# A row softmax on one core: five pieces per tile for four, with the scaling shared by VectorE and ScalarE

## The chip, the core and the metric

The kernel runs on one core of a Trainium2 chip. The metric is the device time of one execution in microseconds (us). The engines that compute here are VectorE (DVE in the profile) and ScalarE (ACT). SyncE (SP) computes nothing; it issues the transfers between the chip's main memory and SBUF, the on-chip memory of 128 partitions. Each engine runs its own list of instructions in order, and the engines wait for each other through semaphores. The transfers of SyncE's queue are worked off by sixteen DMA engines.

## The reference

The input is 16 x 256 rows of 32768 float32 numbers. Each row is divided by the temperature, which is 1.0 here, and put through a softmax:

```python
scaled = logits / temperature
scaled = scaled - scaled.max(axis=-1, keepdims=True)
exp_scaled = np.exp(scaled)
return (exp_scaled / exp_scaled.sum(axis=-1, keepdims=True)).astype(np.float32)
```

That is 537 MB read and 537 MB written, with one exponential for each number.

## The kernel before

A row of 32768 is cut into two halves, and each half lies on a partition of its own. So the 4096 rows become 8192 half rows of `_W` = 16384 columns, and these make `G` = 64 tiles of 128 partitions. A tile is 8.4 MB. SBUF holds three of them in one tensor `X`, which the profile calls xs (`_BUFS` = 3, tile g in slot g modulo 3), and everything is computed in place.

`compute(g)` (line 120) writes down the work of a tile. It treats the tile as `K` = 4 pieces of `_PIECE` = 4096 columns.

- Line 133: VectorE takes the negated maximum of each piece into the small tensor `t`. The first of these waits for the tile's load.
- Line 146: ScalarE takes the exponential of the piece in place, with that maximum as bias, and adds up the piece's sum on the way (the accumulator read that the profile shows as an instruction of its own).
- Lines 157 to 186 join the pieces. A shuffle fetches the numbers of the neighbouring partition, which holds the other half of the row (157). VectorE takes the maximum over all pieces of the row (161). ScalarE turns the differences of the maxima into a factor for each piece, `ee` (168). VectorE multiplies factors and sums and adds them up (174), and takes the reciprocal into `row` (186).
- Line 193: VectorE multiplies each piece in place by its factor and by the reciprocal, as two per-partition scalars of one instruction.

`Stream` wraps an engine with a semaphore: `done` counts an instruction, `wait` makes the engine wait for counts, and leaves out what it has waited for before. `hist` holds, for each tile, the instructions that the tile two later must wait for, as the small tensors exist twice.

`transfers(n)` (line 61) is the order of the transfers, all issued by SyncE: three loads first, then store and load by turns. In the steady part the plan reads: load i, store i-1, load i+1, store i. A load (line 214) waits until the store of the tile three before has finished, since it uses its slot. A store (line 223) waits for the scaling of all pieces that it covers (`overlapping`). Most transfers are a whole tile. Tile 0's store and tile 3's load come in halves, and the last tile is stored in quarters of `_LAST_STORE` = 4096 columns.

Of the kernel before, what the change touches and what calls it, by code (L numbers as in the profile page):

```python
# [7 lines left out]

_W = 16384
_BUFS = 3  # L10
_PIECE = 4096
_LAST_STORE = 4096


class Stream:


    def __init__(self, nc, engine, name):
        self.engine = engine
        self.sem = nc.alloc_semaphore(name)  # L20
        self.count = 0
        self.seen = {}
# [38 lines left out]
def transfers(n):  # L61
    half = _W // 2
    whole = [(0, _W)]
    halves = [(0, half), (half, half)]
    quarters = [(s, _LAST_STORE) for s in range(0, _W, _LAST_STORE)]
    plan = [("L", 0, whole), ("L", 1, whole), ("L", 2, whole)]
    plan += [("S", 0, halves), ("L", 3, halves), ("S", 1, whole), ("S", 2, whole)]
    for i in range(4, n - 2):
        plan += [("L", i, whole), ("S", i - 1, whole)]
    plan += [("L", n - 2, whole), ("L", n - 1, whole)]  # L70
    plan += [("S", n - 3, whole), ("S", n - 2, whole), ("S", n - 1, quarters)]
    return plan


@with_exitstack
def kernel(
    ctx: ExitStack,
    tc: tile.TileContext,
    logits: bass.AP,
    temperature: bass.AP,  # L80
    out: bass.AP,
):
    nc = tc.nc
    inv_t = 1.0 / float(temperature)
    P = nc.NUM_PARTITIONS
    fp32 = mybir.dt.float32
    Exp = mybir.ActivationFunctionType.Exp
    A = mybir.AluOpType

    xf = logits.flatten_outer_dims()  # L90
    of = out.flatten_outer_dims()
    N, V = xf.shape
    assert V == 2 * _W and (N * 2) % P == 0
    x = xf.rearrange("n (h v) -> (n h) v", h=2)
    o = of.rearrange("n (h v) -> (n h) v", h=2)
    G = N * 2 // P
    K = _W // _PIECE
    swap = [i ^ 1 for i in range(32)]

    ctx.enter_context(tc.tile_critical())  # L100
    X = nc.alloc_sbuf_tensor("xs", [P, _BUFS * _W], fp32)
    T = [nc.alloc_sbuf_tensor(f"t{q}", [P, 4 * K], fp32) for q in range(2)]
    E = [nc.alloc_sbuf_tensor(f"ee{q}", [P, 2 * K], fp32) for q in range(2)]
    J = [nc.alloc_sbuf_tensor(f"junk{q}", [P, 2 * K], fp32) for q in range(2)]
    R = [nc.alloc_sbuf_tensor(f"row{q}", [P, 4], fp32) for q in range(2)]

    sp = Stream(nc, nc.sync, "sp")
    dve = Stream(nc, nc.vector, "dve")
    act = Stream(nc, nc.scalar, "act")
    loads = Lanes(nc, "ld")  # L110
    stores = Lanes(nc, "st")
    landed = {}
    stored = {}
    scaled = {}
    hist = {}

    def overlapping(parts, s, n):
        return [token for (a, m), token in parts.items() if a < s + n and s < a + m]

    def compute(g):  # L120
        base = (g % _BUFS) * _W
        t, e, j_, r = T[g % 2], E[g % 2], J[g % 2], R[g % 2]
        tv = t[:, 0 : 4 * K].rearrange("p (a b k) -> p a b k", a=2, b=2)
        old = hist.get(g - 2)
        if old:
            dve.wait(*old)
        sums = None
        for k in range(K):
            s = k * _PIECE
            xs = X[:, base + s : base + s + _PIECE]  # L130
            dve.wait(*overlapping(landed[g], s, _PIECE))
            m = dve.done(
                nc.vector.tensor_reduce(  # L133
                    out=t[:, k : k + 1], in_=xs, axis=mybir.AxisListType.X, op=A.max, negate=True
                )
            )
            if inv_t != 1.0:
                dve.wait(m)
                m = dve.done(
                    nc.vector.tensor_scalar_mul(  # L140
                        out=t[:, k : k + 1], in0=t[:, k : k + 1], scalar1=inv_t
                    )
                )
            act.wait(m)
            sums = act.done(
                nc.scalar.activation(  # L146
                    out=xs,
                    in_=xs,
                    func=Exp,
                    bias=t[:, k : k + 1],  # L150
                    scale=inv_t,
                    accum_out=t[:, K + k : K + k + 1],
                )
            )
        dve.wait(sums)
        sh = dve.done(
            nc.vector.stream_shuffle(out=t[:, 2 * K : 4 * K], in_=t[:, 0 : 2 * K], mask=swap)  # L157
        )
        dve.wait(sh)
        mx = dve.done(  # L160
            nc.vector.tensor_reduce(  # L161
                out=r[:, 0:1], in_=tv[:, :, 0, :], axis=mybir.AxisListType.XY, op=A.min
            )
        )
        act.wait(mx)
        ev = e[:, 0 : 2 * K].rearrange("p (a k) -> p a k", a=2)
        ee = act.done(
            nc.scalar.activation(  # L168
                out=ev, in_=tv[:, :, 0, :], func=Exp, bias=r[:, 0:1], scale=-1.0
            )  # L170
        )
        dve.wait(ee)
        tr = dve.done(
            nc.vector.tensor_tensor_reduce(  # L174
                out=j_[:, 0 : 2 * K].rearrange("p (a k) -> p a k", a=2),
                in0=ev,
                in1=tv[:, :, 1, :],
                scale=1.0,
                scalar=0.0,
                op0=A.mult,  # L180
                op1=A.add,
                accum_out=r[:, 1:2],
            )
        )
        dve.wait(tr)
        rc = dve.done(nc.vector.reciprocal(out=r[:, 2:3], in_=r[:, 1:2]))  # L186
        dve.wait(rc)
        scaled[g] = {}
        for k in range(K):
            s = k * _PIECE  # L190
            xs = X[:, base + s : base + s + _PIECE]
            scaled[g][s, _PIECE] = dve.done(
                nc.vector.tensor_scalar(  # L193
                    out=xs,
                    in0=xs,
                    scalar1=e[:, k : k + 1],
                    scalar2=r[:, 2:3],
                    op0=A.mult,
                    op1=A.mult,
                )  # L200
            )
        hist[g] = (ee, tr)

    for what, g, parts in transfers(G):
        base = (g % _BUFS) * _W
        rows = slice(g * P, (g + 1) * P)
        if what == "L":
            landed[g] = {}
            for k, (s, n) in enumerate(parts):
                if g >= _BUFS:  # L210
                    sp.wait(*overlapping(stored[g - _BUFS], s, n))
                landed[g][s, n] = loads.add(
                    (g % _BUFS, k),
                    nc.sync.dma_start(out=X[:, base + s : base + s + n], in_=x[rows, s : s + n]),
                )
            compute(g)
        else:
            stored[g] = {}
            for k, (s, n) in enumerate(parts):
                sp.wait(*overlapping(scaled[g], s, n))  # L220
                stored[g][s, n] = stores.add(
                    (g % _BUFS, k),
                    nc.sync.dma_start(out=o[rows, s : s + n], in_=X[:, base + s : base + s + n]),  # L223
                )
    sp.wait(*stores.tokens())
# [35 lines left out]
```

## Time and profile before

| What | Value |
|---|---|
| Median of 3 runs | 2512.25 us (2511.07 to 2513.49) |
| The profiled execution's own time | 2513.76 us |
| Its span in the profile | 2512.0 us |
| Mean rate of the transfers over the span | 427 GB/s |
| Bytes moved | 1073.86 MB |
| Load, from issue to landing, median of 63 | 46.1 us |
| Whole-tile store, from issue to landing, median of 62 | 26.7 us |

The busy times of the engines are sums over the whole span. A group's row shows the source line, the engine, the operation, what it writes and reads, the number of instructions, then busy time in us and the mean of one in ns, and last how long the engine had sat idle just before such instructions and who ended that. A row of the timeline shows start and duration in us, with equal neighbours merged (x4 is four instructions). A row of a window shows its ends, its length, the busy time of each engine with its instructions, the clock, the share of the DMA engines' time, and GB/s. A packet of the DMA counts where it starts, so short windows are coarse. SPq is the queue of SyncE.

### The profile page before, as it was taken

How to read it: one execution, taken by the hardware profiler on the slowest of the kernel's cores; microseconds unless marked ns; L12 is line 12 of the kernel's file. 1: busy time of each engine (PE TensorE's matmuls, PEld its weight loads, DVE VectorE, ACT ScalarE, POOL GpSimd, SP SyncE). 2: the span in 40 equal slices, each digit the busy share in tenths (PEclk: the TensorE clock that was granted, in tenths of full speed). 3: DMA queues.
4: the chain of work that ended last, by engine and by line, in shares of the span. 5: the costliest groups of instructions: out<-in, count | busy, mean ns of one | idle time of the engine just before them, and what ended most of it. 6: DMA issues, size and time to landing. Idle time of an engine off the chain costs nothing.

```text
span 2512.0 us, 1661 instructions
## 1 busy us (share of the span) xinstructions
DVE 1755.7 (70%) x896; ACT 993.5 (40%) x577; POOL 0.2 (0%) x4
## 2 busy tenths in 40 slices
DVE  5866676766767667677676766777767676676776
ACT  3443342433424334243342433424334244342443
POOL 0000000000000000000000000000000000000000
DMA  9999999999999999999999999999999999999999
GB/s 409 443 427 432 434 432 432 425 432 432 420 433 425 429 431 422 432 424 430 433 421 431 434 427 425 434 431 422 433 432 421 431 422 433 433 420 432 434 420 389
DMA packets 19165, 1073.86 MB, mean 427 GB/s; under 512 B 2128, under 2 KB 2128, under 8 KB 2128
## 3 DMA queue, kind: packets, MB, share of 16 engines
q1 hardware_dynamic: 19152, 1073.75, 99.8%
q14 instruction: 13, 0.11, 0.0%
HBM read 536.87 MB, written 536.87 MB: 427 GB/s over the span
## 4 chain that ended last, share of the span: by engine, by line
DMA 57%; DVE 36%; ACT 5%; SPq 0%; issue 0%
DMA xs<-in_logits_dram 56%; DVE t L133 23%; DVE xs L193 12%; ACT xs L146 5%; DMA out_dram<-xs 1%; ACT ee L168 0%; SPq L223 0%; DVE row L186 0%; DVE row L161 0%; DVE t L157 0%; DVE junk L174 0%; DVE row L174 0%; SPq L256 0%; SPq L100 0%
## 5 line engine op out<-in xcount | busy, mean ns | idle before, releaser
L146 ACT ACTIVATE xs<-xs,t 128x4096 f32<-128x4096 f32 x256 | 949.2, 3708 | 1464.4 <-DVE t L133 1464.4
L133 DVE TENSOR_REDUCE t<-xs 128x1 f32<-128x4096 f32 x256 | 1113.4, 4412 | 462.1 <-DMA xs<-in_logits_dram 462.1
L193 DVE TENSOR_SCALAR xs<-xs,ee,row 128x4096 f32<-128x4096 f32 x256 | 600.4, 2409 | 2.3
L157 DVE LOAD_MASK_SELECT t<-t x64 | 0.9, 14 | 248.1 <-ACT xs L146 248.1
L146 ACT ACTIVATION_READ_ACCUMULATOR xs<-xs,t 128x1 f32 x256 | 47.7, 186 | 0.0
L168 ACT ACTIVATE ee<-t,row 128x8 f32<-128x8 f32 x64 | 19.2, 301 | 27.6 <-DVE row L161 27.6
L174 DVE CUSTOM_DVE_ANT_1 junk<-ee,t 128x8 f32<-128x8 f32 x64 | 10.7, 167 | 23.6 <-ACT ee L168 23.6
L186 DVE RECIPROCAL row<-row 128x1 f32<-128x1 f32 x64 | 10.5, 164 | 2.2
L161 DVE TENSOR_REDUCE row<-t 128x1 f32<-128x8 f32 x64 | 10.3, 161 | 2.2
L157 DVE STREAM_SHUFFLE t<-t 128x8 f32<-128x8 f32 x64 | 10.2, 160 | 0.0
L174 DVE DVE_READ_ACCUMULATOR2_ANT row<- 128x1 f32 x64 | 5.3, 83 | 0.0
L146 ACT ACT_TABLE_LOAD x1 | 1.3, 1283 | 0.9 <-SPq L100 0.9
L242 POOL MEMSET const-bfloat16-1.0<- 128x1 bf16 x1 | 0.1, 101 | 0.0
L242 POOL MEMSET const-uint8-127<- 128x1 uint8 x1 | 0.1, 101 | 0.0
L242 POOL MEMSET const-float32-0.0<- 128x1 f32 x1 | 0.1, 98 | 0.2 <-issue 0.2
L242 POOL MEMSET const-float32-1.0<- 128x1 f32 x1 | 0.1, 98 | 0.0
## 6 DMA issues: line engine op xcount, KB each, us to landing
out_dram<-xs SPq DMA_DIRECT2D x2, 4096.0 KB, 25.1
xs<-in_logits_dram SPq DMA_DIRECT2D x2, 4096.0 KB, 19.3
out_dram<-xs SPq DMA_DIRECT2D x4, 2048.0 KB, 10.8
xs<-in_logits_dram SPq DMA_DIRECT2D x63, 46.1
out_dram<-xs SPq DMA_DIRECT2D x62, 26.7
```

The lines of the kernel that those rows point to most:

```text
L133: nc.vector.tensor_reduce(out=t[:, k : k + 1], in_=xs, axis=mybir.AxisListType.X, op=A.max, negate=True)
L146: nc.scalar.activation(out=xs, in_=xs, func=Exp, bias=t[:, k : k + 1], scale=inv_t, accum_out=t[:, K + k : K + k + 1],)
L157: nc.vector.stream_shuffle(out=t[:, 2 * K : 4 * K], in_=t[:, 0 : 2 * K], mask=swap)
L161: nc.vector.tensor_reduce(out=r[:, 0:1], in_=tv[:, :, 0, :], axis=mybir.AxisListType.XY, op=A.min)
L168: nc.scalar.activation(out=ev, in_=tv[:, :, 0, :], func=Exp, bias=r[:, 0:1], scale=-1.0)
L174: nc.vector.tensor_tensor_reduce(out=j_[:, 0 : 2 * K].rearrange("p (a k) -> p a k", a=2), in0=ev, in1=tv[:, :, 1, :], scale=1.0, scalar=0. ...
L186: rc = dve.done(nc.vector.reciprocal(out=r[:, 2:3], in_=r[:, 1:2]))
L193: nc.vector.tensor_scalar(out=xs, in0=xs, scalar1=e[:, k : k + 1], scalar2=r[:, 2:3], op0=A.mult, op1=A.mult,)
L242: nc = _bacc.Bacc("TRN2", target_bir_lowering=False, num_devices=1)
```

## The change

Each tile is treated as five pieces, of 4096, 4096, 4096, 2560 and 1536 columns. The maxima and exponentials run over these five. After the reciprocal, a new small VectorE instruction multiplies the five factors by it, into the tensor `junk` (128x5). The scaling then multiplies each piece by this one product: pieces 0, 1 and 4 on VectorE, pieces 2 and 3 on ScalarE (`_ON_ACT`), side by side. A store waits for whichever of the two engines its pieces need. The small tensors grow from four entries to five for each group, and `hist` now also holds the scaling instructions. The plan of transfers, their sizes and the buffers are as before. `compute` is divided into the methods of a class `Tile`, called in the same order.

```diff
-_PIECE = 4096
+_PIECES = (4096, 4096, 4096, 2560, 1536)
+_ON_ACT = (2, 3)
...
-    K = _W // _PIECE
+    K = len(_PIECES)
+    starts = [sum(_PIECES[:k]) for k in range(K)]
...
+        def piece(self, k):
+            s = self.base + starts[k]
+            return X[:, s : s + _PIECES[k]]
+
+        def exponentials(self, k):
+            t = self.t
+            if k == 0 and self.g >= 2:
+                dve.wait(*hist[self.g - 2])
+            xs = self.piece(k)
+            dve.wait(*overlapping(landed[self.g], starts[k], _PIECES[k]))
...
-        for k in range(K):
-            s = k * _PIECE
-            xs = X[:, base + s : base + s + _PIECE]
-            scaled[g][s, _PIECE] = dve.done(
-                nc.vector.tensor_scalar(
-                    out=xs,
-                    in0=xs,
-                    scalar1=e[:, k : k + 1],
-                    scalar2=r[:, 2:3],
-                    op0=A.mult,
-                    op1=A.mult,
-                )
-            )
-        hist[g] = (ee, tr)
+        def scale(self):
+            f = self.j
+            w = dve.done(
+                nc.vector.tensor_scalar_mul(out=f[:, 0:K], in0=self.e[:, 0:K], scalar1=self.r[:, 2:3])
+            )
+            act.wait(w)
+            dve.wait(w)
+            for k in range(K):
+                xs = self.piece(k)
+                if k in _ON_ACT:
+                    token = act.done(nc.scalar.mul(out=xs, in_=xs, mul=f[:, k : k + 1]))
+                else:
+                    token = dve.done(
+                        nc.vector.tensor_scalar_mul(out=xs, in0=xs, scalar1=f[:, k : k + 1])
+                    )
+                scaled[self.g][starts[k], _PIECES[k]] = token
+            hist[self.g] += tuple(scaled[self.g].values())
+
+    def compute(g):
+        a = Tile(g)
         for k in range(K):
...
+            a.exponentials(k)
+        a.totals()
+        a.scale()
```

More of the change, by code (lines that the diff above doesn't have):

```diff
@@ L96 @@
     G = N * 2 // P
-    K = _W // _PIECE
+    K = len(_PIECES)
+    starts = [sum(_PIECES[:k]) for k in range(K)]
+    assert sum(_PIECES) == _W
     swap = [i ^ 1 for i in range(32)]
@@ L118, in overlapping, with __init__ @@
         return [token for (a, m), token in parts.items() if a < s + n and s < a + m]
[L120 to L127, printed above, removed]
-        for k in range(K):
-            s = k * _PIECE
-            xs = X[:, base + s : base + s + _PIECE]
-            dve.wait(*overlapping(landed[g], s, _PIECE))
+    class Tile:
+        def __init__(self, g):
+            self.g = g
+            self.base = (g % _BUFS) * _W
+            self.t, self.e, self.j, self.r = T[g % 2], E[g % 2], J[g % 2], R[g % 2]
+            self.tv = self.t[:, 0 : 4 * K].rearrange("p (a b k) -> p a b k", a=2, b=2)
+            self.sums = None
+            scaled[g] = {}
+        def piece(self, k):
[7 more added lines that the diff above has]
+            dve.wait(*overlapping(landed[self.g], starts[k], _PIECES[k]))
             m = dve.done(
@@ L144, in compute @@
             act.wait(m)
-            sums = act.done(
+            self.sums = act.done(
                 nc.scalar.activation(
@@ L154, in compute @@
             )
-        dve.wait(sums)
-        sh = dve.done(
-            nc.vector.stream_shuffle(out=t[:, 2 * K : 4 * K], in_=t[:, 0 : 2 * K], mask=swap)
-        )
[L159 to L162, printed above, removed]
-            )
-        )
[L165 to L179, printed above, removed]
-                op0=A.mult,
[L181 to L191, printed above, removed]
-            scaled[g][s, _PIECE] = dve.done(
-                nc.vector.tensor_scalar(
-                    out=xs,
-                    in0=xs,
-                    scalar1=e[:, k : k + 1],
-                    scalar2=r[:, 2:3],
-                    op0=A.mult,
-                    op1=A.mult,
-                )
-            )
-        hist[g] = (ee, tr)
+        def totals(self):
+            t, e, r, tv = self.t, self.e, self.r, self.tv
+            dve.wait(self.sums)
+            sh = dve.done(
+                nc.vector.stream_shuffle(out=t[:, 2 * K : 4 * K], in_=t[:, 0 : 2 * K], mask=swap)
+            )
+            dve.wait(sh)
+            mx = dve.done(
+                nc.vector.tensor_reduce(
+                    out=r[:, 0:1], in_=tv[:, :, 0, :], axis=mybir.AxisListType.XY, op=A.min
+                )
+            )
+            act.wait(mx)
+            ev = e[:, 0 : 2 * K].rearrange("p (a k) -> p a k", a=2)
+            ee = act.done(
+                nc.scalar.activation(
+                    out=ev, in_=tv[:, :, 0, :], func=Exp, bias=r[:, 0:1], scale=-1.0
+                )
+            )
+            dve.wait(ee)
+            tr = dve.done(
+                nc.vector.tensor_tensor_reduce(
+                    out=self.j[:, 0 : 2 * K].rearrange("p (a k) -> p a k", a=2),
+                    in0=ev,
+                    in1=tv[:, :, 1, :],
+                    scale=1.0,
+                    scalar=0.0,
+                    op0=A.mult,
+                    op1=A.add,
+                    accum_out=r[:, 1:2],
+                )
+            )
+            dve.wait(tr)
+            rc = dve.done(nc.vector.reciprocal(out=r[:, 2:3], in_=r[:, 1:2]))
+            dve.wait(rc)
+            hist[self.g] = (ee, tr)
@@ new lines, in scale @@
+        def scale(self):
+            f = self.j
+            w = dve.done(
+                nc.vector.tensor_scalar_mul(out=f[:, 0:K], in0=self.e[:, 0:K], scalar1=self.r[:, 2:3])
+            )
+            act.wait(w)
[7 more added lines that the diff above has]
+                        nc.vector.tensor_scalar_mul(out=xs, in0=xs, scalar1=f[:, k : k + 1])
+                    )
+                scaled[self.g][starts[k], _PIECES[k]] = token
+            hist[self.g] += tuple(scaled[self.g].values())
@@ L204 @@
+    def compute(g):
+        a = Tile(g)
+        for k in range(K):
+            a.exponentials(k)
+        a.totals()
+        a.scale()
     for what, g, parts in transfers(G):
```

## The prediction, made before the changed kernel ran

> **What bounds the kernel now.** I read the page's shares and transfer rows first, then the grouped waits, then one tile in the timeline, then the DMA rate in long windows, and last the end of the run.
>
> ```profile
> span 2512.0 us, 1661 instructions
> DVE 1755.7 (70%) x896; ACT 993.5 (40%) x577; POOL 0.2 (0%) x4
> q1 hardware_dynamic: 19152, 1073.75, 99.8%
> L146 ACT ACTIVATE xs<-xs,t 128x4096 f32<-128x4096 f32 x256 | 949.2, 3708 | 1464.4 <-DVE t L133 1464.4
> L133 DVE TENSOR_REDUCE t<-xs 128x1 f32<-128x4096 f32 x256 | 1113.4, 4412 | 462.1 <-DMA xs<-in_logits_dram 462.1
> L193 DVE TENSOR_SCALAR xs<-xs,ee,row 128x4096 f32<-128x4096 f32 x256 | 600.4, 2409 | 2.3
> L168 ACT ACTIVATE ee<-t,row 128x8 f32<-128x8 f32 x64 | 19.2, 301 | 27.6 <-DVE row L161 27.6
> L186 DVE RECIPROCAL row<-row 128x1 f32<-128x1 f32 x64 | 10.5, 164 | 2.2
> L161 DVE TENSOR_REDUCE row<-t 128x1 f32<-128x8 f32 x64 | 10.3, 161 | 2.2
> SPq L223 <- DVE xs L193: 2385.7, 68, 47.6
> ```
>
> The only data queue is busy for 99.8% of sixteen engines' span, while VectorE works 70% and ScalarE 40%. So 0.2% of 2512.0, about 5 us, is all the idle DMA time there is. The last row, SyncE's wait for the scaling, looks alarming (2385.7 us) but is only the place where an early engine parks. Whether it costs anything is read from one tile:
>
> ```profile
> 2355.05 17.40 DVE L133 TENSOR_REDUCE t<-xs 128x1 f32<-128x4096 f32 x4 [7.07 <-DMA xs<-in_logits_dram]
> 2359.50 3.71 ACT L146 ACTIVATE xs<-xs,t 128x4096 f32<-128x4096 f32 x1 [21.35 <-DVE t L133]
> 2372.48 3.71 ACT L146 ACTIVATE xs<-xs,t 128x4096 f32<-128x4096 f32 x1 [0.53 <-DVE t L133]
> 2376.10 0.19 ACT L146 ACTIVATION_READ_ACCUMULATOR xs<-xs,t 128x1 f32 x1
> 2376.33 0.16 DVE L157 STREAM_SHUFFLE t<-t 128x8 f32<-128x8 f32 x1
> 2377.26 0.16 DVE L186 RECIPROCAL row<-row 128x1 f32<-128x1 f32 x1
> 2377.46 9.38 DVE L193 TENSOR_SCALAR xs<-xs,ee,row 128x4096 f32<-128x4096 f32 x4
> 2386.86 0.33 SPq L223 DMA_DIRECT2D out_dram<-xs  x1
> 2387.24 0.43 SPq L214 DMA_DIRECT2D xs<-in_logits_dram  x1
> 2394.01 4.42 DVE L133 TENSOR_REDUCE t<-xs 128x1 f32<-128x4096 f32 x1 [7.17 <-DMA xs<-in_logits_dram]
> ```
>
> A tile takes 2386.86 - 2355.05 = 31.81 us from landing to store. At that moment the previously issued load is still coming: it lands 7.15 us later, and VectorE idles those 7.17 us. The store and the next load join a queue that is not empty. So the period is set by transfers, and compute has 7 us to spare as the last DMA engine sees it.
>
> The early engines may see less. The rate falls after some twelve tiles:
>
> ```profile
> 161.73 8.75 DVE L133 TENSOR_REDUCE t<-xs 128x1 f32<-128x4096 f32 x2 [12.07 <-DMA xs<-in_logits_dram]
> 473.79 8.75 DVE L133 TENSOR_REDUCE t<-xs 128x1 f32<-128x4096 f32 x2 [6.84 <-DMA xs<-in_logits_dram]
> 2432.70 8.74 DVE L133 TENSOR_REDUCE t<-xs 128x1 f32<-128x4096 f32 x2 [6.91 <-DMA xs<-in_logits_dram]
> 161.70:473.70 312.00, 139.19 (x32) 1.00 1.00 434
> 473.70:2432.60 1958.90, 869.89 (x200) 1.00 1.00 428
> ```
>
> The windows hold 32 and 200 reductions, 8 and 50 tiles. From landing to landing a tile takes (473.79 - 161.73)/8 = 39.01 us early and (2432.70 - 473.79)/50 = 39.18 later: 0.17 us a tile, 8.5 us over fifty. The rate falls by more, 434 to 428 GB/s. I read this so: some engines run ahead of the slowest (bytes move faster than tiles land) until their lead has used up the 7 us, then they too find the queue empty at each store. From there all go at the pace of the slowest, which never idle. The end of the run supports it:
>
> ```profile
> 2464.41 8.74 DVE L133 TENSOR_REDUCE t<-xs 128x1 f32<-128x4096 f32 x2
> 2486.81 9.38 DVE L193 TENSOR_SCALAR xs<-xs,ee,row 128x4096 f32<-128x4096 f32 x4
> 2485.00:2489.00 4.00, 2.85 (x7) 0.94 (x3) 0.00 (x0) 1.00 0.27 115
> 2489.00:2509.00 20.00, 7.19 (x4) 0.00 (x0) 0.00 (x0) 1.00 0.96 406
> ```
>
> For 4 us before the last tile's first quarter is scaled (2486.81 + 2.4 = 2489.2) the DMA share is 0.27: about four of sixteen engines are still storing the tile before, the others have run dry.
>
> **The change part by part.** Times below run from a tile's landing.
>
> *Reductions (VectorE).* Three of 4096 columns remain, one becomes 2560 + 1536. The step between them now is (17.40 - 4.42)/3 = 4.33. A column costs (4412 - 161)/(4096 - 8) = 1.040 ns, so 2560 columns take 2.82 and 1536 take 1.75, and back to back 0.09 is overlapped. End: 3 x 4.33 + 2.73 + 1.75 = 17.47, 0.07 later than 17.40.
>
> *Exponentials (ScalarE).* A column costs (3708 - 301)/4088 = 0.833 ns: 2.43 and 1.57 us, and 0.10 more with the accumulator read. The third starts at 3 x 4.33 + 0.12 = 13.11 and ends with its read at 16.92. The fourth is ready at 15.8 but waits for ScalarE, 16.94 to 19.47; the fifth runs 19.49 to 21.16. So the short last piece buys hardly anything: the shuffle starts at 21.20, against 2376.33 - 2355.05 = 21.28 now.
>
> *Totals.* Shuffle to scaling takes 2377.46 - 2376.33 = 1.13. The operands have ten columns for eight, nothing at 1 ns a column. The product of factors on 128x5 is new, priced as its neighbour the reciprocal with the step after it: 0.20. Scaling starts at 22.53.
>
> *Scaling.* VectorE keeps two pieces of 4096, steps of (9.38 - 2.41)/3 = 2.32, and one of 1536: a column costs (2409 - 164)/4095 = 0.548 ns, hence 1.01. It ends at 22.53 + 5.65 = 28.18. That it has one scalar operand for two I take as free; were it as dear as the reduction of the same width, 4.41 a piece, VectorE would end at 33.1. ScalarE's multiply is not in this trace. The nearest row is its exponential of the same shape: 3.71 + 2.43 = 6.14, no accumulator. Bounds: VectorE's own price below (2.41 + 1.57 = 3.98), twice the exponential above (12.28). I take 6.14, same engine and same tile: ScalarE ends at 28.70.
>
> *Table.* The changed program still has a single table load. The multiply would otherwise cost two 1283 ns loads a tile, 2.6 us, and the store would leave at 31.3.
>
> ```profile
> L146 ACT ACT_TABLE_LOAD x1 | 1.3, 1283 | 0.9 <-SPq L100 0.9
> ```
>
> *Store and queue.* SyncE now waits for both engines and issues at 28.72, 3.1 us earlier than 31.81. The transfers and their order are the same. Queued behind that wait is the next load; it moves up with the store. VectorE's new wait for the tile two before is long met; ScalarE is free 6 us after scaling starts, while the next tile's first maximum is 4.4 us after VectorE's 5.65, so nothing queues there.
>
> *Where the 3.1 us go.* Into VectorE's idle time before the first reduction: 39.15 - 28.72 = 10.4 for 7.2. The slowest engines move the same packets, which gives 0. The early engines gain 3.1 us of lead before they run dry. In eight to ten tiles they used some 7, so 3.1 buys about 5 tiles at the early pace: 5 x 0.17 = 0.9 us. Bounds: 0, and all fifty tiles, 8.5.
>
> *Start.* The first tiles run back to back on VectorE and get faster, but behind a full queue:
>
> ```profile
> 86.28 34.84 DMA out_dram<-xs
> ```
>
> That store takes 34.84 us to land where a transfer alone takes half a period, 19.6; some 15 us of work lay ahead of it. Issuing it earlier gains 0.
>
> *End.* The last tile starts its reductions at 2432.70 + 28.2 = 2460.9 for 2464.41, its first quarter is ready 22.53 + 2.41 later at 2485.8, and the hole shrinks from 4 us to under 1. That gains 0 if the four engines still storing decide the end, and at most 3.3 if they do not. I take 0.
>
> Sum: the profiled execution took 2513.76 (span 2512.0 and 1.76 around it), so 2512.9 by this working. It lies 1.5 above the median of the runs; there the forecast is 2512.25 - 0.9 = **2511.4**.
>
> One page speaks against moving a multiply: the Trainium skill, "ScalarE: Activation LUTs", section "Rules for kernel authors", sends multiplications to VectorE and away from ScalarE. The rows agree on the price (2409 against 3708 ns). By that rule all five pieces on VectorE would end at 22.53 + 3 x 2.32 + 1.48 + 1.01 = 32.0, later than 28.7 side by side; an estimate of either lies within the 7 us.
>
> **The rivals.**
>
> *A, running dry is itself the brake.* If the loss after the twelfth tile comes from the dry queue and not from the slow engines, 3.1 us of slack end it: 8.5 us, with the hole's 3.3, 2512.25 - 11.8 = 2500.5. For it: the rate falls just when the lead is spent. Against it: load after load lands 7 us after the store's issue, so its last engine was never without work, and 3.1 us of lead are spent again within a few tiles.
>
> The Trainium skill, "DMA: Bandwidth & Descriptors", section "Latency and other measured facts", expects laggards (engines 7 and 15) only for software descriptor generation. With none here, all sixteen would share the hole and the end would gain its 3.3 us. The queue is a hardware one, and the share of 0.27 disagrees.
>
> *B, slower: both engines writing xs slow the transfers.* For 5.65 us a tile VectorE and ScalarE would both read and write 4096-column pieces in place, which never happens now.
>
> ```profile
> 239.84:257.24 17.40, 17.39 (x4) 11.40 (x6) 0.00 (x0) 1.00 0.99 429
> 262.24:271.64 9.40, 9.38 (x4) 0.00 (x0) 0.00 (x0) 1.00 1.03 446
> 271.64:279.20 7.56, 0.00 (x0) 0.00 (x0) 0.00 (x0) 1.00 0.95 399
> ```
>
> One early tile: 429 GB/s while both engines work, 446 with VectorE's scaling alone. Taken at face value that is 3.8%, 0.215 us a tile, 13.8 us in all: 2526. It decides as soon as the transfers themselves lengthen, since they set the period. Against it: with both engines idle the rate is lowest, 399, so the contrast is packet counting.
>
> *C, the change does not do what it says.* If ScalarE's multiply costs twice the exponential, the store leaves at 34.9, 3.1 us later than now; 4 us of slack remain on the slowest engines, the early pace of eight tiles is lost (8 x 0.17 = 1.4), and the time is 2513.7, within the bound for no change.
>
> **How the numbers follow.** Forecast 0.80, A 0.11, B 0.05, C 0.04. A measurement of this kernel tells about 0.2% from no change, 5.0 us: below 2507.2 is faster, above 2517.3 slower. The forecast's own range is 2508.0 (0.9 and the hole's 3.3) to 2513.9. The range I give goes up to 2515.5, for C and the runs' scatter of 1.2 either way, and down to 2503.0, most of the way to A. Faster: A and 0.01 of the forecast, 0.12. Slower: B with 0.02 for the tails, 0.07. Same: 0.81.
>
> **What would show it.** Right: stores 28 to 29 us after landing; ScalarE's 4096-column multiply near 3.7 us and SyncE waiting for it; VectorE idle about 10.4 us before its first reduction; early period 39.0 and later 39.15 to 39.2, the fall coming some five tiles later; the last hole shorter with the end where it was. Wrong: a later period under 39.1 (A) or an early one over 39.2 (B); stores later than 31.8 (C); a second table load.

## The result, and the profile after

| | Median, us | Runs |
|---|---|---|
| Kernel before | 2513.61 | 7, from 2511.07 to 2514.89 |
| Changed kernel | 2501.14 | 7, from 2497.5 to 2506.28 |

The ratio is 0.9954 with a 95% interval of 0.994 to 0.9968: the change takes 12.5 us off. The prediction said 2511.4 and a range from 2503.0, so the time lies outside, where rival A had put it (2500.5). The changed kernel also scatters more, over 8.8 us where the other has 3.8. The profiled execution took 2506.1 and lies at the upper end, so what it gains in the views below is smaller than the median's gain.

First lines of the changed kernel's page, its groups kept apart by shape, and the longest wait of SyncE's queue (line 32 is the wait inside `Stream`).

```profile
span 2504.3 us, 2045 instructions
DVE 1529.5 (61%) x960; ACT 1390.5 (56%) x833; POOL 0.2 (0%) x4
q1 hardware_dynamic: 19152, 1073.75, 99.7%
L217 DVE TENSOR_SCALAR xs<-xs,junk 128x4096 f32<-128x4096 f32 x128 | 295.4, 2351 | 2.3
L214 ACT ACTIVATE xs<-xs,junk 128x4096 f32<-128x4096 f32 x64 | 237.4, 3709 | 45.5 <-DVE junk L207 45.5
L214 ACT ACTIVATE xs<-xs,junk 128x2560 f32<-128x2560 f32 x64 | 154.5, 2414 | 0.0
L157 ACT ACT_TABLE_LOAD x1 | 1.3, 1283 | 0.9 <-SPq L103 0.9
SPq L32 <- ACT xs L214: 2267.7, 61, 47.7
```

ScalarE's multiply costs what its exponential costs, 3709 ns, there is one table load, and SyncE now waits for ScalarE. The DMA share is the same as before, 99.7% for 99.8%: by this number nothing happened. It counts a packet as busy time however long it takes, which will matter below. One tile in the timeline of the changed kernel:

```profile
2112.11 17.46 DVE L144 TENSOR_REDUCE t<-xs 128x1 f32<-128x4096 f32 x5 [11.20 <-DMA xs<-in_logits_dram]
2131.34 1.56 ACT L157 ACTIVATE xs<-xs,t 128x1536 f32<-128x1536 f32 x1
2133.03 0.16 DVE L171 STREAM_SHUFFLE t<-t 128x10 f32<-128x10 f32 x1
2134.18 0.23 DVE L207 TENSOR_SCALAR junk<-ee,row 128x5 f32<-128x5 f32 x1
2134.44 5.55 DVE L217 TENSOR_SCALAR xs<-xs,junk 128x4096 f32<-128x4096 f32 x3
2134.44 6.03 ACT L214 ACTIVATE xs<-xs,junk 128x4096 f32<-128x4096 f32 x2 [0.71 <-DVE junk L207]
2140.55 0.33 SPq L248 DMA_DIRECT2D out_dram<-xs  x1
2151.22 17.46 DVE L144 TENSOR_REDUCE t<-xs 128x1 f32<-128x4096 f32 x5 [11.23 <-DMA xs<-in_logits_dram]
```

The store leaves 2140.55 - 2112.11 = 28.44 us after landing, against 31.81 before and 28.72 forecast. The load on its way lands 10.67 us later, against 7.15.

Where the gain lies along the run is read from the landings. The first column is the start of a tile's first reduction. Tiles 4, 24 and 62 of the changed kernel, then tile 24 of the kernel before (its tiles 4 and 62 are in the prediction, 161.73 and 2432.70):

```profile
160.35 17.46 DVE L144 TENSOR_REDUCE t<-xs 128x1 f32<-128x4096 f32 x5 [26.31 <-DMA xs<-in_logits_dram]
940.79 17.46 DVE L144 TENSOR_REDUCE t<-xs 128x1 f32<-128x4096 f32 x5 [11.09 <-DMA xs<-in_logits_dram]
2424.00 17.46 DVE L144 TENSOR_REDUCE t<-xs 128x1 f32<-128x4096 f32 x5 [10.81 <-DMA xs<-in_logits_dram]
```

```profile
945.31 17.40 DVE L133 TENSOR_REDUCE t<-xs 128x1 f32<-128x4096 f32 x4 [7.13 <-DMA xs<-in_logits_dram]
```

From tile 4 to 24 the period is (940.79 - 160.35)/20 = 39.02 us for 39.18 before, from 24 to 62 it is 39.03 for 39.14. The small differences add up: tile 62 lands 8.7 us sooner, of which 1.4 were there at tile 4. From there to the end it takes 80.3 us for 79.3, so the end gives 1.0 back.

The rate over time, in windows of the kernel before and then of the changed one (the last column is GB/s):

```profile
161.00:520.00 359.00, 253.07 (x128) 141.20 (x82) 0.00 (x0) 1.00 1.00 433
520.00:1000.00 480.00, 338.69 (x171) 194.42 (x113) 0.00 (x0) 1.00 1.00 427
1000.00:1500.00 500.00, 347.72 (x181) 193.62 (x114) 0.00 (x0) 1.00 1.00 429
2000.00:2400.00 400.00, 280.37 (x142) 156.57 (x91) 0.00 (x0) 1.00 1.00 428
```

```profile
161.00:520.00 359.00, 221.78 (x137) 198.18 (x118) 0.00 (x0) 1.00 1.00 433
520.00:1000.00 480.00, 297.03 (x184) 272.70 (x165) 0.00 (x0) 1.00 1.00 432
1000.00:1500.00 500.00, 306.06 (x193) 274.72 (x165) 0.00 (x0) 1.00 1.00 431
2000.00:2400.00 400.00, 248.64 (x153) 225.63 (x135) 0.00 (x0) 1.00 1.00 430
```

Both begin at 433. The kernel before falls to 427 after 520 us; the changed one stays at 432 and 431 until 1500 us and ends at 430. The fall comes twelve to twenty-five tiles later, not five, and is smaller.

The end of the changed kernel, in windows:

```profile
2465.00:2485.00 20.00, 10.68 (x12) 13.99 (x9) 0.00 (x0) 1.00 0.85 365
2485.00:2495.00 10.00, 0.00 (x0) 0.00 (x0) 0.00 (x0) 1.00 0.99 421
2495.00:2500.00 5.00, 0.00 (x0) 0.00 (x0) 0.00 (x0) 1.00 0.53 226
2500.00:2504.30 4.30, 0.00 (x0) 0.00 (x0) 0.00 (x0) 1.00 0.08 32
```

Most DMA engines are done soon after 2495, some only after 2500. The sixteen finish the last quarter within 5.5 us of each other, in the kernel before within 0.7. The end waits for the last of them; it gained nothing here.

### The profile page after: what moved, and what is told of

Read it like the earlier page. It is cut to its first block, busy times and chain, and to the rows that moved or that the text cites. A ratio compares the mean times of both kernels' runs of the same rounds, so it can differ in the third digit from the quotient of the medians.

```text
span 2504.3 us, 2045 instructions
## 1 busy us (share of the span) xinstructions
DVE 1529.5 (61%) x960; ACT 1390.5 (56%) x833; POOL 0.2 (0%) x4
## 2 busy tenths in 40 slices
DMA packets 19169, 1073.89 MB, mean 429 GB/s; under 512 B 2128, under 2 KB 2128, under 8 KB 2128
## 3 DMA queue, kind: packets, MB, share of 16 engines
q1 hardware_dynamic: 19152, 1073.75, 99.7%
## 4 chain that ended last, share of the span: by engine, by line
DMA 60%; DVE 19%; ACT 18%; another core or an unknown queue 1%; issue 0%; SPq 0%
DMA xs<-in_logits_dram 57%; DVE t L144 17%; ACT xs L157 10%; ACT xs L214 7%; DMA out_dram<-xs 3%; DVE xs L217 1%; ACT ee L182 0%; SPq L248 0%; DVE junk L207 0%; DVE row L200 0%; DVE row L175 0%; DVE t L171 0%; DVE junk L188 0%; DVE row L188 0%
## 5 line engine op out<-in xcount | busy, mean ns | idle before, releaser
L144 DVE TENSOR_REDUCE t<-xs 128x1 f32<-128x4096 f32 (+2 forms) x320 | 1117.3, 3558 | 696.0 <-DMA xs<-in_logits_dram 696.0
L157 ACT ACTIVATE xs<-xs,t 128x4096 f32<-128x4096 f32 (+2 forms) x320 | 966.0, 3019 | 1015.4 <-DVE t L144 1015.4
L214 ACT ACTIVATE xs<-xs,junk 128x4096 f32<-128x4096 f32 (+1 forms) x128 | 385.9, 3062 | 45.5 <-DVE junk L207 45.5
L217 DVE TENSOR_SCALAR xs<-xs,junk 128x4096 f32<-128x4096 f32 (+1 forms) x192 | 355.0, 1906 | 2.3
L157 ACT ACTIVATION_READ_ACCUMULATOR xs<-xs,t 128x1 f32 x320 | 59.6, 186 | 0.0
L182 ACT ACTIVATE ee<-t,row 128x10 f32<-128x10 f32 x64 | 19.5, 305 | 27.9 <-DVE row L175 27.9
L188 DVE CUSTOM_DVE_ANT_1 junk<-ee,t 128x10 f32<-128x10 f32 x64 | 10.9, 170 | 23.8 <-ACT ee L182 23.8
L207 DVE TENSOR_SCALAR junk<-ee,row 128x5 f32<-128x5 f32 x64 | 14.8, 231 | 2.2
L175 DVE TENSOR_REDUCE row<-t 128x1 f32<-128x10 f32 x64 | 10.5, 164 | 2.2
L171 DVE STREAM_SHUFFLE t<-t 128x10 f32<-128x10 f32 x64 | 10.4, 162 | 0.0
```

The source lines that it names most:

```text
L144: nc.vector.tensor_reduce(out=t[:, k : k + 1], in_=xs, axis=mybir.AxisListType.X, op=A.max, negate=True)
L157: nc.scalar.activation(out=xs, in_=xs, func=Exp, bias=t[:, k : k + 1], scale=inv_t, accum_out=t[:, K + k : K + k + 1],)
L175: nc.vector.tensor_reduce(out=r[:, 0:1], in_=tv[:, :, 0, :], axis=mybir.AxisListType.XY, op=A.min)
L182: nc.scalar.activation(out=ev, in_=tv[:, :, 0, :], func=Exp, bias=r[:, 0:1], scale=-1.0)
L188: nc.vector.tensor_tensor_reduce(out=self.j[:, 0 : 2 * K].rearrange("p (a k) -> p a k", a=2), in0=ev, in1=tv[:, :, 1, :], scale=1.0, scala ...
L207: nc.vector.tensor_scalar_mul(out=f[:, 0:K], in0=self.e[:, 0:K], scalar1=self.r[:, 2:3])
```

## The experiments

Two theories stood after the result. *Slack*: the time follows from how long before the last queued transfer ends the next store is issued, and nothing else of the change matters. *Its rivals*: the sharing between engines, or the finer pieces, or transfers that differ with them. "Store at" below is the time from a tile's landing to its store, read from each timeline. All runs of the kernel before beside these had medians of 2513.3 to 2514.6.

**1. The change with its store late again.**

```diff
             dve.wait(rc)
+            dve.done(
+                nc.vector.tensor_reduce(
+                    out=r[:, 3:4], in_=X[:, self.base : self.base + 3200],
+                    axis=mybir.AxisListType.X, op=A.max,
+                )
+            )
             hist[self.g] = (ee, tr)
```

> The changed kernel, with one more VectorE reduction over 3200 columns (about 3.4 us, its result is not used) between the reciprocal and the factors. The store leaves about 31.8 us after landing again, as before the change, while pieces, engines and arithmetic of the change stay. Slack theory (the time follows from how long before the last queued transfer ends the next store is issued): 2513 us, within 3 of the kernel before, VectorE idle about 7.2 us before its first reduction. Rival (the gain comes from ScalarE taking over part of the in-place writing, or from the finer pieces): it stays near 2501. The prediction's own step (3.1 us of slack buy 0.9 us) cannot tell here, it would allow either number within 1 us of the other.

Measured: 2514.27 us (11 runs), ratio 1.0005 (0.9996 to 1.0013). The whole gain is gone with nothing else undone. In the timeline of this run the store left 2110.11 and the load on its way landed 7.54 us later:

```profile
2100.35 3.49 DVE L203 TENSOR_REDUCE row<-xs 128x1 f32<-128x3200 f32 x1
2110.11 0.33 SPq L256 DMA_DIRECT2D out_dram<-xs  x1
2117.65 17.46 DVE L144 TENSOR_REDUCE t<-xs 128x1 f32<-128x4096 f32 x5 [8.10 <-DMA xs<-in_logits_dram]
```

**2. Four pieces, shared.**

```diff
-_PIECES = (4096, 4096, 4096, 2560, 1536)
+_PIECES = (4096, 4096, 4096, 4096)
```

> The changed kernel with four pieces of 4096, the last two scaled by ScalarE. Computed from the rows: scaling starts 22.6 us after landing, two ScalarE pieces of 3.71 end at 30.0 us, so the store leaves 1.6 us later than in the changed kernel and 1.8 us earlier than before. Slack theory: between the two kernels, about 2506 (2503 to 2510). Rival (the five pieces matter): 2512 or more. Rival (sharing the scaling between the engines matters, not the time of the store): 2501.

Measured: store at 30.0, 2510.56 us (12 runs, 2500.05 to 2512.91), ratio 0.9977 (0.9968 to 0.9987). Between the two kernels as expected, though 0.6 above the expected span. Sharing alone does not give 2501.

**3. The kernel before, its store later still.**

```diff
         dve.wait(rc)
+        late = dve.done(
+            nc.vector.tensor_reduce(
+                out=r[:, 3:4], in_=X[:, base : base + 3200],
+                axis=mybir.AxisListType.X, op=A.max,
+            )
+        )
+        dve.wait(late)
         scaled[g] = {}
```

> The kernel before, with one more VectorE reduction over 3200 columns (about 3.5 us, its result is not used) ahead of the scaling: the store leaves about 35.3 us after landing. Slack theory: slower again by about as much as the change gained, 2525 us (2519 to 2532), the rate falling below 434 GB/s within the first few tiles. The prediction's theory (the slowest DMA engines set the pace and always have work, the store still leaves 3.7 us before they run dry): 2513.7, at most 1.4 us more.

Measured: store at 35.3, 2543.96 us, ratio 1.0123 (1.011 to 1.0136). The direction is that of the slack theory, and the prediction's theory allowed 1.4 us. But the size, 29.4 us, is more than twice the 12 expected and outside the expected span. Tiles 4, 24 and 62, and two windows at the start:

```profile
171.11 17.40 DVE L133 TENSOR_REDUCE t<-xs 128x1 f32<-128x4096 f32 x4 [7.32 <-DMA xs<-in_logits_dram]
952.52 17.40 DVE L133 TENSOR_REDUCE t<-xs 128x1 f32<-128x4096 f32 x4 [3.52 <-DMA xs<-in_logits_dram]
2454.97 17.40 DVE L133 TENSOR_REDUCE t<-xs 128x1 f32<-128x4096 f32 x4 [3.46 <-DMA xs<-in_logits_dram]
```

```profile
100.00:116.00 16.00, 11.65 (x10) 13.23 (x9) 0.00 (x0) 1.00 1.06 459
116.00:126.00 10.00, 9.96 (x4) 0.00 (x0) 0.00 (x0) 1.00 0.24 106
```

9.4 us are a hole at the start: the first tiles run back to back, the store of tile 2 comes late and the DMA share is 0.24 for ten microseconds (tile 4 lands at 171.11 for 161.73). The period of the later tiles is (2454.97 - 952.52)/38 = 39.54 us for 39.14, which makes 15.1 us more by tile 62. The end takes 85.8 us from there for 79.3, 6.5 more, and the tiles from 4 to 24 took 2.2 less. The rate falls mostly later than in the first few tiles: it is 432 GB/s from 161 to 520 us, 428 until 1000 and 424 after that.

**4. Five pieces, all on VectorE.**

```diff
-_ON_ACT = (2, 3)
+_ON_ACT = ()
```

> The changed kernel with all five pieces scaled by VectorE: the piece sizes of the change alone. Computed from the rows: 22.6 plus 3 x 2.32 plus 1.4 plus 1.0, the store leaves about 31.9 us after landing. Slack theory: 2513, as before, within 3. Rival (piece sizes matter): nearer 2501.

Measured: store at 31.6, 2512.23 us (11 runs), ratio 0.9993 (0.9984 to 1.0001). The pieces by themselves do nothing that can be told from no change: the interval holds 1.

**5. No scaling at all.**

```diff
         for k in range(K):
-            s = k * _PIECE
-            xs = X[:, base + s : base + s + _PIECE]
-            scaled[g][s, _PIECE] = dve.done(
-                nc.vector.tensor_scalar(
...
+            scaled[g][k * _PIECE, _PIECE] = rc
```

> The kernel before with the scaling left out (line 193): a store waits for the reciprocal alone and writes the unscaled exponentials. The store leaves about 22.5 us after landing, with VectorE alone and four pieces as before. Slack theory: the gain goes on beyond the changed kernel, the rate stays near 434 GB/s to the end, 2490 us (2484 to 2497). If slack helps only up to the changed kernel's 28.4 us: 2500 (2497 to 2506). The prediction's theory (the slowest DMA engines set the pace): 2511.

Measured: store at 22.4, 2488.78 us (4 runs), ratio 0.99 (0.9885 to 0.9915). Tiles 4, 24 and 62, and a window:

```profile
160.74 17.40 DVE L133 TENSOR_REDUCE t<-xs 128x1 f32<-128x4096 f32 x4 [45.34 <-DMA xs<-in_logits_dram]
938.93 17.40 DVE L133 TENSOR_REDUCE t<-xs 128x1 f32<-128x4096 f32 x4 [16.22 <-DMA xs<-in_logits_dram]
2407.27 17.40 DVE L133 TENSOR_REDUCE t<-xs 128x1 f32<-128x4096 f32 x4 [16.24 <-DMA xs<-in_logits_dram]
```

```profile
2000.00:2400.00 400.00, 181.23 (x106) 158.87 (x93) 0.00 (x0) 1.00 1.00 434
```

The first twenty periods are 38.91 us, the last 38 are 38.64, and the rate is still 434 GB/s at the end. A tile has landed when the last DMA engine is done, so no DMA engine is slow by nature: given slack, the laggards run at the pace of the others. This run also spares VectorE the scaling; run 9 shows that this is not what helps.

**6 and 7. Slack from the other side: loads in halves**, for the changed kernel and for the kernel before.

```diff
-    plan = [("L", 0, whole), ("L", 1, whole), ("L", 2, whole)]
+    plan = [("L", 0, halves), ("L", 1, halves), ("L", 2, halves)]
...
-        plan += [("L", i, whole), ("S", i - 1, whole)]
-    plan += [("L", n - 2, whole), ("L", n - 1, whole)]
+        plan += [("L", i, halves), ("S", i - 1, whole)]
+    plan += [("L", n - 2, halves), ("L", n - 1, halves)]
```

> The changed kernel with every load issued as two halves, one right after the other; the first half lands about 9.8 us sooner and its maxima run under the second. The store leaves about 20 us after the second half has landed, 8.5 us sooner than in the changed kernel. Slack theory: 2490 (2483 to 2497). Rival (each issue of a transfer costs: half as many again): slower than the changed kernel, 2505 or more.

> The kernel before with every load issued as two halves, VectorE scaling four pieces alone as before. The store leaves about 23.1 us after the second half has landed (31.8 less two reductions). Slack theory: like the run without scaling, 2491 (2484 to 2498), better than the change without any of its parts. Rival (sharing the scaling is what helps): 2511.

Measured: 2494.78 us with the change, ratio 0.9924 (0.9912 to 0.9937), and 2493.58 without it, ratio 0.9919 (0.9905 to 0.9933), both within what was expected of slack. The kernel before with its loads in halves is faster than the changed kernel and has nothing of the change; with the halves, the change adds 1.2 us. One tile of it:

```profile
1200.71 8.74 DVE L133 TENSOR_REDUCE t<-xs 128x1 f32<-128x4096 f32 x2 [6.84 <-DMA xs<-in_logits_dram]
1210.39 8.75 DVE L133 TENSOR_REDUCE t<-xs 128x1 f32<-128x4096 f32 x2 [0.94 <-DMA xs<-in_logits_dram]
1233.56 0.34 SPq L223 DMA_DIRECT2D out_dram<-xs  x1
```

Two reductions run before the second half has landed, and the store leaves 23.2 us after that landing with all the scaling still on VectorE. These two runs change the packets of the loads as well, from 64 to 32 KB. No run has halves with a late store, so how much of their gain is slack, and how much the smaller packets, is not shown by them alone.

**8. One late store in a run with ample slack**, tile 32 of the run without scaling.

```diff
         dve.wait(rc)
+        if g == 32:
+            for k in range(6):
+                rc = dve.done(
+                    nc.vector.tensor_reduce(
+                        out=r[:, 3:4], in_=X[:, base : base + 4096],
+                        axis=mybir.AxisListType.X, op=A.max,
+                    )
+                )
+                dve.wait(rc)
         scaled[g] = {}
```

> The run without scaling, with six more VectorE reductions of 4096 columns (26 us, results not used) ahead of the reciprocal's use in tile 32 alone. That one store is late enough for all sixteen DMA engines to run dry, some 11 us by the slowest, so that they start again in step. Spread theory (engines that work in step slow each other where they switch between load and store; slack only keeps the spread that they have gained): from tile 35 on the landing period goes back from 38.64 to about 39.1 us for some ten tiles, as it was at the start, and the time is 2505 us (2501 to 2510). Depth theory (a queue of 16 us is enough to keep the packets fast): the period is 38.64 again at once, 2499 us or less.

Measured: 2508.87 us (10 runs), ratio 0.9982 (0.9973 to 0.9991). Tile 31, the late reductions of tile 32, and tiles 35 and 45:

```profile
1211.69 17.40 DVE L133 TENSOR_REDUCE t<-xs 128x1 f32<-128x4096 f32 x4 [16.25 <-DMA xs<-in_logits_dram]
1272.73 26.69 DVE L191 TENSOR_REDUCE row<-xs 128x1 f32<-128x4096 f32 x6
1380.69 17.40 DVE L133 TENSOR_REDUCE t<-xs 128x1 f32<-128x4096 f32 x4 [16.39 <-DMA xs<-in_logits_dram]
1770.33 17.40 DVE L133 TENSOR_REDUCE t<-xs 128x1 f32<-128x4096 f32 x4 [16.73 <-DMA xs<-in_logits_dram]
```

Four tiles take 1380.69 - 1211.69 = 169.0 us, 14.4 more than four periods of 38.64. The ten periods after that are (1770.33 - 1380.69)/10 = 38.96 us although VectorE again idles 16 us before each tile. So the depth theory falls: a deep queue does not by itself keep the packets fast. What was lost is the spread between the DMA engines (first table below). But this is not the loss that the change removed, as the second table shows.

**9. Halves without scaling**, edits 5 and 7 together.

> The kernel before with loads in halves and the scaling left out (line 193). If the 4.8 us between the run with halves (2493.6) and the run without scaling (2488.8) are the price of the smaller packets: 2493 (2491 to 2495), although the store now leaves some 14 us after landing. If they are slack still missing: 2488.5.

Measured: 2493.39 us, ratio 0.9919 (0.9905 to 0.9932), the same as with scaling. The 4.8 us above the run without scaling are the price of the halves, not missing slack. And where the store is early enough, it makes no difference whether the engines scale or not, so run 5 did not gain by sparing them that work.

**10. The changed kernel with half of the scaling.**

```diff
-                if k in _ON_ACT:
+                if k in (1, 2):
+                    token = w
+                elif k in _ON_ACT:
```

> The changed kernel with pieces 1 and 2 left unscaled: VectorE scales pieces 0 and 4, ScalarE piece 3, the store leaves about 25.8 us after landing, 2.6 us sooner than in the changed kernel and 3.3 us later than without scaling. Spread theory (the slack of the run without scaling, 16 us, is more than its largest spread of about 9 us needs): nearly all of the rest is gained here, 2491 us (2488 to 2495). A straight line between the two runs would give 2495.6.

Measured: store at 25.6, 2495.93 us (5 runs, 2490.76 to 2499.23), ratio 0.9925 (0.9911 to 0.9938). The expected 2491 is missed, the straight line's 2495.6 is what came, though the five runs reach over both. No sharp point shows from which slack is enough.

**The spread itself.** Each of the sixteen DMA engines closes its share of a transfer with a packet of 4 bytes (2128 of them for 133 transfers). The time from the first to the last of such sixteen is the lead of the first engine over the last. Here it is in us, as the mean of the four transfers around six times of the run:

```
lead of first over last   340    540    860   1220   1700   2400
run 3, store later        0.8    1.1    2.6    2.5    2.8    2.6
before                    4.2    5.9    5.9    5.8    5.3    5.2
changed                   4.0    5.8    7.9    8.5    8.6    8.6
run 10, half scaled       3.9    5.8    7.9    9.1   10.2   11.0
run 5, no scaling         3.8    5.5    6.9    7.1    7.1    7.1
run 8, one late           1.3    2.6    5.8    8.1    2.8    6.5
```

The lead grows until the next store comes only just in time for the first engine. Between 1000 and 2400 us, when a store is issued, the first engine still has 1.2 us of work on the load that is coming in the kernel before, and 1.4 in the changed one (medians). That is less than one packet of 64 KB, which takes 2.418 us. Without scaling 8.7 us are left, and the lead stops by itself.

**Where the time is lost.** A packet on an engine starts where the one before it ended, 2.414 us after that one's start. The sixteen packets of a tile so take 38.62 us. The second table has what an engine spends beyond that in the same stretch, in us a tile and as the mean of the sixteen: time of packets above 2.418 us, on the last packet of its share of a store, of a load, and on others, and idle time. (Slow is a packet over 2.618 us; it is the last one if a 4-byte packet starts within 25 ns of its end; idle time is from packets put into sixteen chains, and rough.) The sum with 38.62 meets the period measured from landing to landing:

```
            store at   store's last   load's last   other   idle    sum   measured
run 3         35.3         0.41          0.05       0.13    0.32   39.53    39.53
before        31.8         0.30          0.11       0.08    0.07   39.18    39.17
run 1         31.8         0.28          0.11       0.08    0.04   39.13    39.14
run 4         31.6         0.29          0.04       0.11    0.03   39.10    39.10
run 2         30.0         0.27          0.15       0.08    0.05   39.16    39.15
changed       28.4         0.18          0.16       0.05    0.02   39.03    39.04
run 10        25.6         0.04          0.07       0.02    0.01   38.76    38.82
run 5         22.4         0.00          0.00       0.01    0.00   38.63    38.64
```

So the later the store, the more time goes into the last packets of stores (0.00 to 0.41 us a tile); only run 4 is out of order, by 0.01. An engine stands idle for hardly any time except in run 3. Slack also puts the loss off: run 2 is no better in this stretch than the kernel before, but its tiles 4 to 24 take 39.04 us each for 39.18. Over the whole profiled execution the packets of an engine take 29.4 us more than 2.418 us each before and 20.3 after the change, which is 9.1 less, while its time without a packet goes from 5.6 to 7.0. Together that is the 7.7 us by which the spans differ. Without scaling it is 4.2 and 4.8. After the late store of run 8 (1380 to 2400 us) the loss is another one: 0.08 us a tile on the last packets of loads and none on those of stores, as at the start of every run of this table (161 to 520 us: 0.07 to 0.15 on loads, at most 0.03 on stores).

## Why the prediction was wrong

**The compute part held.** Reductions end 17.46 us after landing (forecast 17.47), the shuffle starts at 20.92 (21.20), scaling at 22.33 (22.53), VectorE's part takes 5.55 (5.65), ScalarE's 6.03 (6.14). The short last piece bought hardly anything, as said: run 4 shows 31.6 for 31.8. SyncE waits for ScalarE, and there is no second table load.

**Rival C and rival B fell.** The store is 3.4 us earlier (C's own 34.9 adds up to 34.8), and with both engines writing the pieces the rate is 433 GB/s early on, as before. The sign that was named for rival A came: the later period is 39.03 us, under 39.1.

**The step that failed is "Where the 3.1 us go".** It took the pace of the slowest DMA engines as theirs ("the slowest engines move the same packets, which gives 0") and sized the rest as five tiles at the early pace, 0.9 us. The median gained 12.5. Two things were mistaken.

- The slowest engines have no pace of their own. That they always had work was right, and was taken for proof that slack could not help them. But an engine that always has work can still lose time: from 1000 us on, when all engines keep their distance, the period of a tile is 39.17 us before, 39.04 changed and 38.64 without scaling. What differs is the time in slow packets (0.49, 0.39 and 0.01 us a tile), not the idle time (0.07, 0.02 and 0.00). The same holds for the first reading, that 5 us are "all the idle DMA time there is": the number is right, but it was no bound on the gain, as the gain lay in busy time.
- The 3.1 us were taken to be used up in some five tiles at the early pace. The lead of the changed kernel grew for some twelve tiles longer, until about 1000 us, and the loss after that was smaller, so the gain did not end there. Nor did the first engines use up "the 7 us" and find the queue empty: their lead stopped at some 5.5 us, with 1.2 us of work left.

The price for this was on the table. The step's own upper bound was 8.5 us for all fifty tiles, and rival A read the fall from 434 to 428 GB/s as the work of the dry queue and worked out 2500.5. It was given 0.11, because the last engine's idle time spoke against it. The lead of the first engines, and not the last engine's 7 us, was the number to weigh. Rival A had the direction right, but that its sum comes so near the median is partly luck. The hole's 3.3 us did not come, the loss became smaller and did not end, and the queue is hardly ever dry. In the profiled execution 7.7 us were gained; where the other runs of the changed kernel, up to 8.6 us faster, gained theirs, no profile shows.

**The end** was sized as the prediction had it: the hole before the last tile bought nothing. The end even lost 1.0 us in the profiled executions, where it waits for the last engine and the sixteen finish 5.5 us apart for 0.7.

**What stays open.** Why an engine's last packet of a store takes longer when the next store comes late, no run shows; the traces give the packets' times and not what they waited for. Nor is it shown why the last packets of loads are slow in some stretches (0.07 to 0.15 us a tile at the start of every run, 0.16 later in the changed kernel) and not in others (0.00 in run 5 from 1000 us on). It is not simply that engines in step hinder each other: in run 3 the lead stays near 1 us until 540 us, and up to 520 us the stores lose 0.01 us a tile.

## What to carry to other kernels

When a transfer-bound kernel shows its queue 99.8% busy, compare the rate early and late and the rate with ample slack before calling it done. This one lost 25 us (1%, 2513.9 for 2488.8) to packets that took longer when the next store came late, and the DMA share showed 99.8% in both. Count slack from the first DMA engine to finish, not from the last to land. The largest gain in a version that computes the whole softmax came from the transfers (loads in halves, 2493.58 us), not from the engines' work.

## What the runs showed of the hardware

- Sixteen DMA engines with equal work drifted apart by 5 to 9 us (3 in run 3, 11 in run 10) and mostly stayed so, on the queue that the profile calls hardware_dynamic. The Trainium skill, "DMA: Bandwidth & Descriptors", section "Latency and other measured facts", names engines 7 and 15 as usually slower, with a best guess at the cause that is specific to software descriptor generation. These runs show laggards without it; which engines they are the traces do not tell.
- Slow packets are mostly an engine's last packet of a transfer, though only one in eight is a last one: 400 of the 444 over 2.618 us in the kernel before, 365 of 403 in the changed one (1000 to 2400 us).
- A late store goes on costing after its delay. One late store in the run without scaling cost 20.1 us (2508.87 for 2488.78). In the profiled executions 14.4 us lie between tiles 31 and 35, and another 7.0 between tiles 35 and 62. A store 3.5 us later in each tile made the later periods 0.40 us longer.
- Halving the loads' packets from 64 to 32 KB cost 4.6 us over 64 tiles (2493.39 for 2488.78), with the same bytes.
- The multiply on ScalarE takes what its exponential takes, 3709 and 3708 ns on 128x4096, against 2351 on VectorE. That agrees with the rule of the Trainium skill that the prediction weighed ("ScalarE: Activation LUTs", section "Rules for kernel authors"). Here the dearer engine still shortened the scaling, from 9.38 to 6.03 us, as it worked at the same time.
